# A decoder layer in split fp32: one more summed weight pair in the last gate/up block, two more in the second down block, and other pool lifetimes around them

## The chip, the cores and the metric

The kernel runs on one core of a Trainium2 chip. The metric is the device time of one execution in microseconds; "the time" below is the median of several runs, and single executions are named as such. The core has a matrix engine (PE, with its weight loads shown as PEld), a vector engine (DVE), a scalar engine (ACT), a general engine (POOL) and a sync engine (SP) that in this kernel issues most of the weight transfers.

## The reference

One layer of a hybrid decoder on 256 tokens of width 2048, all in float32:

```python
u = rmsnorm(h)
# one combined projection, then two groups of heads
lru_x, lru_gate, q, k, v, ret_gate = split(u @ w_in)
A = rg_lru(causal_conv(lru_x)) * gelu(lru_gate)
B = group_norm(retention(rope(q), rope(k), v)) * silu(ret_gate)
h = h + concat(A, B) @ w_out                         # 2048 x 2048
m = rmsnorm(h)
h = h + (silu(m @ w_gate) * (m @ w_up)) @ w_down     # d_ff = 5632, so 11 blocks of 512
out = rmsnorm(h)
```

The change touches only the last two lines of matrix products: the gate/up products and the down product.

## The kernel before, in words

**Precision.** A float32 product is made of three matmuls. Both operands are split into a high part (rounded to the matmul's own type, `F32R`) and a low part (the rest): `three` (in the functions below) adds high x high, high x low and low x high into one PSUM bank. Weights arrive raw: one transfer of 128x1024 floats (512 KB) on SP into a tile `raw`. `split` (L122 to L124) then makes two tiles of it: ACT copies it to `wh` (L123), and DVE subtracts to get `wl` (L124). Where a 512-wide half is split alone the tiles are called `bh` and `bl`. So each weight goes transfer, ACT cast, DVE subtraction, matmul.

**Quads and summed quads.** From the output projection on, the weights are worked in pairs of raw tiles, a `Quad`: a 2x2 grid of blocks `b11`, `b12` (first raw tile) and `b22`, `b21` (second), against a 2x2 grid of activations. A plain quad makes eight block products (`EIGHT`), that is 24 matmuls of 128x512. A summed quad makes seven (`SEVEN`, a scheme of the Strassen-Winograd kind), 21 matmuls; for that DVE first forms sums of weight blocks in place in the raw tiles (`add`, four additions of 128x512, L661), and more splits are made: `b11` alone, the pair `b22`/`b21`, then the two summed tiles. The activations need sums too (`Left` with `sums`: four 128x128 operations and one more split, tiles `s`, `sh`, `sl`), made once for each pair.

**Blocks.** The program is a list of steps. Blocks 0 and 1 are the output projection, 2 to 12 are gate/up, then come two down blocks. In gate/up a summed quad is cut in two steps: `s` is its shared part (class `Shared`, 4 products, 12 matmuls), which is worked during the block ahead, and `d` the rest (class `Direct`, 3 products, 9 matmuls, which loads the second raw tile of that quad once more). `p` is a plain quad and `h` half of one. `SUMMED[b]` says which of the eight quads of block b are summed, and `STEPS[b]` in which order block b takes its own steps and the `s` steps of block b+1. Each down block walks 22 quads in the order `ORDER_DOWN[d]`; those in `SUMMED_DOWN[d]` are summed.

**Buffers.** `raw` has 6 buffers, `split` 4 (each a `wh` and a `wl`), `acts` 60 tiles of 128x512 for activations. From block 3 to the start of block 12 there are two more pools: `raw2` (2 buffers, taken by each fourth raw tile) and `split2` (2, by each third split); `swap` opens them and `stop_more` ends their use. At the end of gate/up `swap_back` closes them and in their place opens `late` (4 tiles, the final norm's weights `fw`) and `resid2` (8 tiles): POOL issues eight transfers `htok<-kept_rows` (256 KB each) that bring the residual rows back, and four for `fw`.

**What sets the order.** Transfers of weights are issued on SP some loads ahead, each when its buffer is released. A scheduler that works in program order by dependencies sets the order on PE, DVE and ACT; the `end` of the second down block alone is in hand-written order on PE. Every engine then works its own list strictly in order, and waits for semaphores of the others. The first and second half of the residual rows belong to the first and second down block: `into` (L919, L920) and `post` (L941) add results to `htok`, and L984 multiplies by `fw`.

Of the kernel before, what the change touches and what calls it, by code (L numbers as in the profile page):

```python
# [9 lines left out]
F32R = mybir.dt.float32r  # L10
# [20 lines left out]

SUMMED = ((), (4, 5), (2, 3), (1, 2, 3)) + ((0, 1, 2, 3),) * 8 + ((1, 2, 3),)
SUMMED_OUT, SUMMED_FFN = (4, 5), (0, 1, 2, 3)

PLAIN = ((4, 5, 6, 7, 0, 1, 2, 3),) * 2 + (tuple(range(8)),) * 11
STEPS = ("pppspppspp", "ppspdpsdpp", "pdpsdpspspp", "pspsdpsdpsdp") + ("psdhsdhsdhsdhp",) * 7 + ("psdpsdpsddp", "psdpsdpsdpp")


EARLY_DOWN = (0, 1, 2)
SUMMED_DOWN = (9, 12, 15, 17, 19), (5, 7, 9, 11, 13, 15, 17)  # L40
ORDER_DOWN = (3, 4, 0, 5, 6, 1, 7, 8, 2) + tuple(range(9, 22)), tuple(range(22))


@with_exitstack
def tile_hymba_layer(ctx: ExitStack, tc: tile.TileContext, A: dict, out: bass.AP):
# [10 lines left out]
    tpool = early.enter_context(tc.tile_pool(name="tmp", bufs=6))  # L56
    late, resid, more, turn_of = [], [xpool], [], [0, 0]
    extra = ExitStack()
# [15 lines left out]
    def split_tiles():  # L74
        turn_of[1] += 1
        pool_ = more[1] if more and turn_of[1] % 3 == 0 else wpool
        return [pool_.tile([P, 1024], F32R, tag=g, name=nm(g)) for g in ("wh", "wl")]

    def raw_tile():
        turn_of[0] += 1  # L80
        pool_ = more[0] if more and turn_of[0] % 4 == 0 else rpool
        return pool_.tile([P, 1024], F32, tag="raw", name=nm("raw"))
# [464 lines left out]
    class Left:  # L547
# [5 lines left out]

        def __init__(self, f, sums):
            self.h, self.l = [act_tile("ah", F32R)], [act_tile("al", F32R)]
            split(self.h[0], self.l[0], f)
            if sums:
                a11, a21, a12, a22 = (f[:, n * P : n * P + P] for n in range(4))
                g = act_tile("s")
                s1, s2, s3, s4 = (g[:, n * P : n * P + P] for n in range(4))  # L560
                v.tensor_tensor(out=s1, in0=a22, in1=a21, op=ALU.subtract)
                v.tensor_tensor(out=s2, in0=a11, in1=s1, op=ALU.add)
                v.tensor_tensor(out=s3, in0=a11, in1=a21, op=ALU.subtract)
                v.tensor_tensor(out=s4, in0=a12, in1=s2, op=ALU.subtract)
                self.h.append(act_tile("sh", F32R))
                self.l.append(act_tile("sl", F32R))
                split(self.h[1], self.l[1], g)
# [49 lines left out]
    class Quad:  # L617
# [5 lines left out]
        def __init__(self, src, sums, before=None):  # L623
            self.src, self.sums, self.before = src, sums, before
            self.parts = {}
            self.apart = False

# [11 lines left out]
        def load(self, half):  # L639
            r = raw_tile()  # L640
            nc.sync.dma_start(out=r, in_=self.src[:, half * 1024 : half * 1024 + 1024])
            if half == 0 and self.before:
                self.before()
            if not self.sums:
                self.cut(("b22", "b21") if half else ("b11", "b12"), r)
                return
            if half == 0:
                self.ra = r
                self.parts["b11"] = act_tile("bh", F32R), act_tile("bl", F32R)
                split(*self.parts["b11"], r[:, :512])  # L650
                return
            self.cut(("b22", "b21"), r)
            self.add(r)
            self.cut(("t1", "t3"), self.ra)
            self.cut(("t2", "t4"), r)
# [31 lines left out]
    def block(index, quads, lefts, post, ps, tail, early={}, ordered=False):  # L687
# [39 lines left out]
        for i in range(n):  # L727
            program.append(([quads[i]], step(i)))

        def end():  # L730
# [29 lines left out]
    class Direct(Quad):  # L760
# [8 lines left out]
        def load(self, half):  # L769
            r = raw_tile()  # L770
            nc.sync.dma_start(out=r, in_=self.src[:, 1024:2048])
# [14 lines left out]
    class Block:  # L786
# [45 lines left out]
        def put(self, after):  # L832
            plain = [i for i in PLAIN[self.index] if i not in self.summed]
            for k, kind in enumerate(self.steps):
                if kind == "p":
                    i, n = plain.pop(0), len(plain)
                    quad = Quad(self.src(i), False)
                    run = lambda i=i, quad=quad, k=k, n=n: self.plain(i, quad, k == 0, n == 0)
                elif kind == "h":
# [63 lines left out]
    def make_left(p):  # L903
        if dl[p] is None:
            dl[p] = Left(ff[p], p in EARLY_DOWN + SUMMED_DOWN[0] + SUMMED_DOWN[1])

# [196 lines left out]
    def stop_more():  # L1103
        more.clear()

    def swap_back():
        extra.close()
        late.append(ctx.enter_context(tc.tile_pool(name="late", bufs=4)))
        resid[0] = ctx.enter_context(tc.tile_pool(name="resid2", bufs=8))
        for key in [(cb, t) for cb in range(4) for t in range(2)]:  # L1110
            htok[key] = res_tile("htok")
            pool.dma_start(out=htok[key], in_=kept[key])
        load_fw()

    blocks = [Block(d, lambda i, d=d: A["w_out"][8 * d + i], y, out_post(d), STEPS[d], SUMMED[d]) for d in range(2)]
# [5 lines left out]
    for b, after in zip(blocks, blocks[1:] + [down]):  # L1121
        if b.index == 3:
            program.append(([], swap))
        if b.index == NB + 1:
            program.append(([], stop_more))
        b.put(after)
    program.append(([], swap_back))

# [119 lines left out]
```

## Time and profile before

| | |
|---|---|
| time, median of 3 runs | 1083.32 us (1082.24 to 1083.6) |
| the profiled execution, its own time | 1082.46 us |
| its span, first to last instruction | 1080.7 us (so 1.76 us lie outside) |
| PE busy | 1070.2 us (99%), 5089 matmuls |
| DVE busy | 964.1 us (89%) |
| ACT busy | 664.5 us (61%) |
| POOL busy | 57.2 us (5%) |
| granted PE clock, mean | 0.998 |

A row of a timeline reads: start in us, busy time in us, engine, line, operation, output<-inputs, shapes, count, and in brackets how long the engine idled before it and what ended that. On PE successive matmuls overlap: a row's busy time is longer than the step from one start to the next. In the chain of work that ended last the times are the steps along it. Block boundaries, by the lines in the trace: the residual transfers of `swap_back` are issued from 824.9 us on, the first down block's results are added to the rows (L941) around 957 to 963 us, and the second down block runs from there to about 1070 us.

### The profile page before, as it was taken

The page shows a single profiled execution, that of the slowest core. Times are in us where ns is not written, and L with a number is a line of the kernel's source. Part 1 is how long each engine was busy: PE and PEld are TensorE (multiplying, and loading weights), DVE is VectorE, ACT ScalarE, POOL GpSimd, SP SyncE. Part 2 cuts the span into 40 slices and gives each one's busy share as a digit, 9 for nine tenths or more (in the row PEclk, how much of TensorE's full clock was granted, in tenths as well). Part 3 has the DMA queues.
Part 4 walks back from the last instruction along what each step waited for, and adds up shares of the span by engine and source line. Part 5 has one row for each costly group of instructions (what it writes and reads, how often), then busy time and mean ns, then how long its engine had stood idle before and what let it go on. Part 6 is the DMA issues. An engine that isn't in the chain of part 4 may idle for free.

```text
span 1080.7 us, 14590 instructions
## 1 busy us (share of the span) xinstructions
PE 1070.2 (99%) x5089; PEld 897.7 (83%) x5089; DVE 964.1 (89%) x1399; ACT 664.5 (61%) x947; POOL 57.2 (5%) x73
## 2 busy tenths in 40 slices
PE   9999999999999999999999999999999999999997
PEld 7888888888888888888888888888888888888886
DVE  7889789988878889989999999999999889997886
ACT  7666644468756676656656565665656656654563
POOL 0602230000000000000000000000002000000001
PEclk9999999999999999999999999999999999999999
DMA  9965475554556588677776777777767856474662
GB/s 325 336 213 171 159 254 166 183 176 158 192 195 234 183 304 273 231 235 256 257 270 228 251 260 242 263 269 232 258 234 270 289 181 214 162 245 159 214 212 101
DMA packets 71386, 244.62 MB, mean 226 GB/s; under 512 B 8208, under 2 KB 8592, under 8 KB 71312
## 3 DMA queue, kind: packets, MB, share of 16 engines
q1 hardware_dynamic: 68400, 236.34, 64.6%
q0 software_dynamic: 1472, 4.72, 1.3%
q10 hardware_dynamic: 1440, 2.62, 0.6%
q8 instruction: 40, 0.66, 0.2%
q14 instruction: 34, 0.28, 0.1%
HBM read 239.46 MB, written 4.19 MB: 225 GB/s over the span
## 4 chain that ended last, share of the span: by engine, by line
PE 98%; DVE 1%; DMA 1%; POOL 0%; SPq 0%; ACT 0%; issue 0%; POOLq 0%; ACTq 0%
PE c L685 22%; PE c L683 22%; PE c L684 22%; PE fm L194 11%; PE fm L196 5%; PE tm L174 3%; PE tm L175 3%; PE tm L176 3%; PE p L683 1%; PE p L685 1%; PE p L684 1%; PE ft L865 1%; DMA x<-in_x 1%; PE ht L588 0%; PE sc L492 0%; DVE wl L124 0%
## 5 line engine op out<-in xcount | busy, mean ns | idle before, releaser
L123 ACT CAST wh<-raw 128x1024 fp32r<-128x1024 f32 (+1 forms) x498 | 462.9, 959 | 323.8 <-PE c L685 130.8
L124 DVE TENSOR_TENSOR wl<-raw,wh 128x1024 fp32r<-128x1024 f32 (+1 forms) x498 | 542.2, 1115 | 72.5 <-ACT wh L123 71.2
L684 PE MATMUL c<-wl,ah 128*128 128x512 f32 x826 | 322.7, 391 | 0.0
L685 PE MATMUL c<-wh,al 128*128 128x512 f32 x826 | 321.8, 390 | 0.0
L683 PE MATMUL c<-wh,ah 128*128 128x512 f32 x826 | 280.3, 391 | 0.0
L683 PEld LDWEIGHTS c<-wh,ah 128*128 128x128 f32 x826 | 155.1, 188 | 32.0 <-ACT wh L123 0.3
L685 PEld LDWEIGHTS c<-wh,al 128*128 128x128 f32 x826 | 155.2, 188 | 31.8
L684 PEld LDWEIGHTS c<-wl,ah 128*128 128x128 f32 x826 | 155.2, 188 | 31.6
L194 PE MATMUL fm<-u,wh 128*128 128x512 f32 x512 | 161.4, 396 | 0.0
L196 PEld LDWEIGHTS fm<-u,wl 128*128 128x128 f32 x512 | 96.1, 188 | 22.4
L196 PE MATMUL fm<-u,wl 128*128 128x256 f32 x512 | 101.2, 279 | 0.0
L661 DVE TENSOR_TENSOR raw<-raw,raw 128x512 f32<-128x512 f32 x114 | 78.4, 689 | 2.0
L661 DVE TENSOR_TENSOR raw<-raw 128x512 f32<-128x512 f32 x114 | 78.3, 688 | 1.4
L194 PEld LDWEIGHTS fm<-u,wh 128*128 128x128 f32 x512 | 78.4, 189 | 0.3
L684 PE MATMUL c<-wl,sh 128*128 128x512 f32 x192 | 74.3, 390 | 0.0
L685 PE MATMUL c<-wh,sl 128*128 128x512 f32 x192 | 73.7, 390 | 0.0
L683 PE MATMUL c<-wh,sh 128*128 128x512 f32 x192 | 67.3, 391 | 0.3 <-ACT sh L123 0.3
L176 PE MATMUL tm<-wh,u 128*128 128x512 f32 x128 | 48.7, 391 | 0.0
L175 PE MATMUL tm<-wl,u 128*128 128x512 f32 x128 | 48.7, 393 | 0.0
L174 PE MATMUL tm<-wh,u 128*128 128x512 f32 x128 | 46.9, 394 | 1.4 <-ACT u L298 1.4
L683 PEld LDWEIGHTS c<-wh,sh 128*128 128x128 f32 x192 | 36.1, 188 | 8.1 <-ACT sh L123 0.7
L685 PEld LDWEIGHTS c<-wh,sl 128*128 128x128 f32 x192 | 36.1, 188 | 7.5
(247 smaller groups left out, 1027.4 us busy)
## 6 DMA issues: line engine op xcount, KB each, us to landing
raw<-in_w_gu SPq DMA_DIRECT2D x216, 512.0 KB, 5.3
raw<-in_w_down SPq DMA_DIRECT2D x91, 512.0 KB, 4.6
raw<-in_w_out SPq DMA_DIRECT2D x34, 512.0 KB, 3.7
raw<-in_w_lx SPq DMA_DIRECT2D x16, 512.0 KB, 6.4
raw<-in_w_k SPq DMA_DIRECT2D x16, 512.0 KB, 3.6
raw<-in_w_q SPq DMA_DIRECT2D x16, 512.0 KB, 4.2
raw<-in_w_rg SPq DMA_DIRECT2D x16, 512.0 KB, 3.5
raw<-in_w_lg SPq DMA_DIRECT2D x16, 512.0 KB, 3.5
```

What stands on the lines that cost most here:

```text
L123: act.copy(out=dst_h, in_=src)
L124: v.tensor_tensor(out=dst_l, in0=src, in1=dst_h.bitcast(F32), op=ALU.subtract)
L174: pe.matmul(ps, ah, wh, start=first, stop=False)
L175: pe.matmul(ps, ah, wl, start=False, stop=False)
L176: pe.matmul(ps, al, wh, start=False, stop=last)
L194: pe.matmul(ps, wh, hl, start=n + i == 0, stop=False)
L196: pe.matmul(ps[:, :S], wl, hl[:, :S], start=False, stop=n + i == len(order) - 1)
L661: v.tensor_tensor(out=dst, in0=a, in1=b, op=ALU.add)
L683: pe.matmul(p, ah, bh, start=first, stop=False, skip_group_check=onto)
L684: pe.matmul(p, ah, bl, start=False, stop=False, skip_group_check=onto)
L685: pe.matmul(p, al, bh, start=False, stop=last, skip_group_check=onto)
L865: pe.transpose(pt[:, o : o + P], g[:, (2 * b + c) * P : (2 * b + c) * P + P], ident)
```

## The change

It does the following.

1. The last gate/up block (12) has four summed quads in place of three; block 11 then takes four `s` steps, and block 12's steps shrink by one.
2. The second down block has nine summed quads in place of seven (12 and 19 are new), in another order: summed ones stand at positions 1, 3, 5, ... 17, plain ones between them. Before, the first five were plain and the summed ones stood at 5, 7, ... 17.
3. `raw2` is taken only by raw tiles that are split at once and not added up (`brief`: those of `Direct`, and the second raw tile of a block's last plain quad), not by each fourth. `split2` is taken as before.
4. The extra pools live longer: `stop_more` comes after step 6 of the first down block, `swap_back` after step 9.
5. The residual rows come back in two halves: `rows_back(0)`, four transfers, in `swap_back`; `rows_back(1)`, four transfers, after step 7 of the second down block. Between the two, a pool `sums` of four tiles holds the `sh` and `sl` tiles of pairs 12 and 19.

The diff, cut to its core:

```diff
-SUMMED = ((), (4, 5), (2, 3), (1, 2, 3)) + ((0, 1, 2, 3),) * 8 + ((1, 2, 3),)
+SUMMED = ((), (4, 5), (2, 3), (1, 2, 3)) + ((0, 1, 2, 3),) * 9
-STEPS = (...) + ("psdhsdhsdhsdhp",) * 7 + ("psdpsdpsddp", "psdpsdpsdpp")
+STEPS = (...) + ("psdhsdhsdhsdhp",) * 8 + ("psdpsdpsddp",)
-SUMMED_DOWN = (9, 12, 15, 17, 19), (5, 7, 9, 11, 13, 15, 17)
-ORDER_DOWN = (3, 4, 0, 5, 6, 1, 7, 8, 2) + tuple(range(9, 22)), tuple(range(22))
+SUMMED_DOWN = (9, 12, 15, 17, 19), (5, 7, 9, 11, 12, 13, 15, 17, 19)
+ORDER_DOWN = (3, 4, 0, 5, 6, 1, 7, 8, 2) + tuple(range(9, 22)), (0, 12, 1, 19, 2, 5, 3, 7, 4, 9, 6, 11, 8, 13, 10, 15, 14, 17, 16, 18, 20, 21)
+BESIDE = (12, 19)
...
-    def raw_tile():
-        turn_of[0] += 1
-        pool_ = more[0] if more and turn_of[0] % 4 == 0 else rpool
+    def raw_tile(brief=False):
+        pool_ = more[0] if more and brief else rpool
...
         def load(self, half):            # Quad
-            r = raw_tile()
+            r = raw_tile(self.brief and half == 1)
...
         for i in range(n):               # block()
             program.append(([quads[i]], step(i)))
+            if i in hooks[ordered]:
+                program.append(([], hooks[ordered][i]))
...
         def load(self, half):            # Direct
-            r = raw_tile()
+            r = raw_tile(True)
...
+                    quad.brief = n == 0  # the last plain quad of a Block
...
-            dl[p] = Left(ff[p], p in EARLY_DOWN + SUMMED_DOWN[0] + SUMMED_DOWN[1])
+            place = sum_tile if p in BESIDE else act_tile
+            dl[p] = Left(ff[p], p in EARLY_DOWN + SUMMED_DOWN[0] + SUMMED_DOWN[1], place)
...
+    def sum_tile(name, dt):
+        return sums_kept[0].tile([P, 512], dt, tag="sum", name=nm(name))
+
+    def rows_back(d):
+        resid[0] = ctx.enter_context(tc.tile_pool(name=f"resid_{d}", bufs=4))
+        for key in [(cb, t) for cb in (2 * d, 2 * d + 1) for t in range(2)]:
+            htok[key] = res_tile("htok")
+            pool.dma_start(out=htok[key], in_=kept[key])
+
     def swap_back():
         extra.close()
+        rows_back(0)
         late.append(ctx.enter_context(tc.tile_pool(name="late", bufs=4)))
-        resid[0] = ctx.enter_context(tc.tile_pool(name="resid2", bufs=8))
-        for key in [(cb, t) for cb in range(4) for t in range(2)]:
-            ...
         load_fw()
+        sums_kept.append(beside.enter_context(tc.tile_pool(name="sums", bufs=4)))
+
+    def sums_end():
+        beside.close()
+        rows_back(1)
+
+    hooks = {0: {6: stop_more, 9: swap_back}, 1: {7: sums_end}}
...
-        if b.index == NB + 1:
-            program.append(([], stop_more))
         b.put(after)
-    program.append(([], swap_back))
```

How it moves the instructions, at three places. In all, PE's list loses 9 rows and DVE's gains 19.

**Start of the second down block, DVE.** In the kernel before, quads 0, 1, 2, ... here are plain. From the split of a plain quad's raw tile (`wl_9238`) on, DVE's list reads (L941 and L984 finish the first block's residual rows):

```order
L124 TENSOR_TENSOR wl_9238<-raw_9235,wh_9237 128x1024
L984 TENSOR_TENSOR htok_8244<-htok_8244,fw_8260 128x512
L984 TENSOR_TENSOR htok_8248<-htok_8248,fw_8262 128x512
L941 TENSOR_TENSOR htok_8250<-c_1664_7918,htok_8250 128x512
L984 TENSOR_TENSOR htok_8246<-htok_8246,fw_8260 128x512
L124 TENSOR_TENSOR wl_9244<-raw_9241,wh_9243 128x1024
L124 TENSOR_TENSOR wl_9278<-raw_9275,wh_9277 128x1024
L984 TENSOR_TENSOR htok_8250<-htok_8250,fw_8262 128x512
L124 TENSOR_TENSOR wl_9284<-raw_9281,wh_9283 128x1024
```

In the changed kernel the second quad of this block is pair 12, summed: its raw tiles are `raw_9177` and `raw_9243`. Behind the split of the second one, `wl_9246`, the list reads (L945, L924 and L988 are the lines that L941, L920 and L984 were):

```order
L945 TENSOR_TENSOR htok_8644<-c_1673_7956,htok_8644 128x512
L924 TENSOR_TENSOR htok_8648<-htok_8648,part_9153 128x512
L124 TENSOR_TENSOR bl_9180<-raw_9177,bh_9179 128x512
L945 TENSOR_TENSOR htok_8648<-c_1672_7952,htok_8648 128x512
L661 TENSOR_TENSOR raw_9177<-raw_9177 128x512
L661 TENSOR_TENSOR raw_9177<-raw_9177,raw_9243 128x512
L988 TENSOR_TENSOR htok_8642<-htok_8642,fw_8653 128x512
L661 TENSOR_TENSOR raw_9243<-raw_9177,raw_9243 128x512
L988 TENSOR_TENSOR htok_8646<-htok_8646,fw_8655 128x512
L988 TENSOR_TENSOR htok_8644<-htok_8644,fw_8653 128x512
L661 TENSOR_TENSOR raw_9243<-raw_9243 128x512
L124 TENSOR_TENSOR wl_9254<-raw_9177,wh_9253 128x1024
```

Before, at most four narrow rows (128x512) stand between two wide subtractions (128x1024). Now eleven do, between `wl_9246` and the first summed tile `wl_9254`: `bl_9180` and the four additions of pair 12 stand among the rows that finish the first block. On PE, from the first use of `wl_9246` to the first use of `wl_9254`, the changed list reads:

```order
L684 MATMUL c_1979_9267<-wl_9246,ah_8672 128x512
L685 MATMUL c_1979_9267<-wh_9245,al_8673 128x512
L684 MATMUL c_1980_9271<-wl_9246,sh_8681 128x512
L685 MATMUL c_1980_9271<-wh_9245,sl_8682 128x512
L684 MATMUL p_1989_9307<-bl_9180,ah_8672 128x512
L685 MATMUL p_1989_9307<-bh_9179,al_8673 128x512
L683 MATMUL p_1990_9317<-wh_9253,sh_8681 128x512
L683 MATMUL p_1989_9307<-bh_9303,ah_9018 128x512
L684 MATMUL p_1990_9317<-wl_9254,sh_8681 128x512
```

So eight matmuls stand from the one use to the other. Before, a whole plain quad (24 matmuls for two wide subtractions) stood at this place.

**The alternation of plain and summed quads, DVE.** Before, in its steady part (from the narrow split `bl_9606` of one summed quad to `bl_9687` of the next):

```order
L124 TENSOR_TENSOR bl_9606<-raw_9603,bh_9605 128x512
L661 TENSOR_TENSOR raw_9603<-raw_9603 128x512
L124 TENSOR_TENSOR wl_9564<-raw_9549,wh_9563 128x1024
L661 TENSOR_TENSOR raw_9603<-raw_9603,raw_9630 128x512
L124 TENSOR_TENSOR wl_9570<-raw_9567,wh_9569 128x1024
L124 TENSOR_TENSOR wl_9600<-raw_9597,wh_9599 128x1024
L124 TENSOR_TENSOR wl_9633<-raw_9630,wh_9632 128x1024
L661 TENSOR_TENSOR raw_9630<-raw_9603,raw_9630 128x512
L124 TENSOR_TENSOR wl_9641<-raw_9603,wh_9640 128x1024
L661 TENSOR_TENSOR raw_9630<-raw_9630 128x512
L124 TENSOR_TENSOR bl_9687<-raw_9684,bh_9686 128x512
```

In the changed kernel, early in the block, from `bl_9389` (pair 5) to the next summed quad's `bl_9470` (pair 7); `raw_9301` and `raw_9332` are pair 19's, `raw_9350` and `raw_9380` plain pair 2's:

```order
L124 TENSOR_TENSOR bl_9389<-raw_9386,bh_9388 128x512
L661 TENSOR_TENSOR raw_9332<-raw_9332 128x512
L124 TENSOR_TENSOR wl_9343<-raw_9301,wh_9342 128x1024
L661 TENSOR_TENSOR raw_9386<-raw_9386 128x512
L124 TENSOR_TENSOR wl_9347<-raw_9332,wh_9346 128x1024
L661 TENSOR_TENSOR raw_9386<-raw_9386,raw_9413 128x512
L124 TENSOR_TENSOR wl_9353<-raw_9350,wh_9352 128x1024
L124 TENSOR_TENSOR wl_9383<-raw_9380,wh_9382 128x1024
L124 TENSOR_TENSOR wl_9416<-raw_9413,wh_9415 128x1024
L124 TENSOR_TENSOR wl_9424<-raw_9386,wh_9423 128x1024
L661 TENSOR_TENSOR raw_9413<-raw_9386,raw_9413 128x512
L124 TENSOR_TENSOR bl_9470<-raw_9467,bh_9469 128x512
```

The plain quad's first raw tile is released by `wl_9570` before and by `wl_9353` in the changed kernel, and its buffer is the one that the next summed quad's load (`raw_9684`, `raw_9467`) waits for. Before, one wide subtraction and two additions stand between the narrow split and that release; now two wide subtractions and three additions do.

**POOL's transfers.** Before, the last of the norm's weights are followed at once by all residual rows:

```order
L893 DMA fw_8264<-in_final_norm_w 128x512
L893 DMA fw_8266<-in_final_norm_w 128x512
L1112 DMA htok_8244<-kept_rows 128x512
L1112 DMA htok_8246<-kept_rows 128x512
L1112 DMA htok_8248<-kept_rows 128x512
L1112 DMA htok_8250<-kept_rows 128x512
```

In the changed kernel:

```order
L1119 DMA htok_8646<-kept_rows 128x512
L1119 DMA htok_8648<-kept_rows 128x512
L896 DMA fw_8653<-in_final_norm_w 128x512
L896 DMA fw_8655<-in_final_norm_w 128x512
L896 DMA fw_8657<-in_final_norm_w 128x512
L896 DMA fw_8659<-in_final_norm_w 128x512
L1119 DMA htok_9579<-kept_rows 128x512
L1119 DMA htok_9581<-kept_rows 128x512
```

The first four residual rows have moved ahead of the norm's weights, and the other four behind them. `htok_9579` waits on PE until the last use of the `sums` tiles, the `sl` of pair 19.

More of the change, by code (lines that the diff above doesn't have):

```diff
@@ L28 @@
 N_SMALL = 104
-SUMMED = ((), (4, 5), (2, 3), (1, 2, 3)) + ((0, 1, 2, 3),) * 8 + ((1, 2, 3),)
+SUMMED = ((), (4, 5), (2, 3), (1, 2, 3)) + ((0, 1, 2, 3),) * 9
 SUMMED_OUT, SUMMED_FFN = (4, 5), (0, 1, 2, 3)
 PLAIN = ((4, 5, 6, 7, 0, 1, 2, 3),) * 2 + (tuple(range(8)),) * 11
-STEPS = ("pppspppspp", "ppspdpsdpp", "pdpsdpspspp", "pspsdpsdpsdp") + ("psdhsdhsdhsdhp",) * 7 + ("psdpsdpsddp", "psdpsdpsdpp")
+STEPS = ("pppspppspp", "ppspdpsdpp", "pdpsdpspspp", "pspsdpsdpsdp") + ("psdhsdhsdhsdhp",) * 8 + ("psdpsdpsddp",)
 EARLY_DOWN = (0, 1, 2)
-SUMMED_DOWN = (9, 12, 15, 17, 19), (5, 7, 9, 11, 13, 15, 17)
-ORDER_DOWN = (3, 4, 0, 5, 6, 1, 7, 8, 2) + tuple(range(9, 22)), tuple(range(22))
+SUMMED_DOWN = (9, 12, 15, 17, 19), (5, 7, 9, 11, 12, 13, 15, 17, 19)
+ORDER_DOWN = (3, 4, 0, 5, 6, 1, 7, 8, 2) + tuple(range(9, 22)), (0, 12, 1, 19, 2, 5, 3, 7, 4, 9, 6, 11, 8, 13, 10, 15, 14, 17, 16, 18, 20, 21)
+BESIDE = (12, 19)
 @with_exitstack
@@ L56, in tile_hymba_layer @@
     tpool = early.enter_context(tc.tile_pool(name="tmp", bufs=6))
-    late, resid, more, turn_of = [], [xpool], [], [0, 0]
+    late, resid, more, turn_of = [], [xpool], [], [0]
     extra = ExitStack()
@@ L74, in split_tiles @@
     def split_tiles():
-        turn_of[1] += 1
-        pool_ = more[1] if more and turn_of[1] % 3 == 0 else wpool
+        turn_of[0] += 1
+        pool_ = more[1] if more and turn_of[0] % 3 == 0 else wpool
         return [pool_.tile([P, 1024], F32R, tag=g, name=nm(g)) for g in ("wh", "wl")]
-    def raw_tile():
-        turn_of[0] += 1
-        pool_ = more[0] if more and turn_of[0] % 4 == 0 else rpool
+    def raw_tile(brief=False):
+        pool_ = more[0] if more and brief else rpool
         return pool_.tile([P, 1024], F32, tag="raw", name=nm("raw"))
@@ L552, in tile_hymba_layer, with __init__ @@
         names = ("a11", "a21", "a12", "a22", "s1", "s2", "s3", "s4")
-        def __init__(self, f, sums):
+        def __init__(self, f, sums, place=act_tile):
             self.h, self.l = [act_tile("ah", F32R)], [act_tile("al", F32R)]
@@ L564, in __init__ @@
                 v.tensor_tensor(out=s4, in0=a12, in1=s2, op=ALU.subtract)
-                self.h.append(act_tile("sh", F32R))
-                self.l.append(act_tile("sl", F32R))
+                self.h.append(place("sh", F32R))
+                self.l.append(place("sl", F32R))
                 split(self.h[1], self.l[1], g)
@@ L625, in __init__ @@
             self.parts = {}
-            self.apart = False
+            self.apart = self.brief = False
         def cut(self, names, raw):
@@ L1104, in stop_more @@
         more.clear()
+    beside, sums_kept = ExitStack(), []
+    def sum_tile(name, dt):
[5 more added lines that the diff above has]
+            pool.dma_start(out=htok[key], in_=kept[key])
     def swap_back():
         extra.close()
+        rows_back(0)
         late.append(ctx.enter_context(tc.tile_pool(name="late", bufs=4)))
-        resid[0] = ctx.enter_context(tc.tile_pool(name="resid2", bufs=8))
-        for key in [(cb, t) for cb in range(4) for t in range(2)]:
-            htok[key] = res_tile("htok")
-            pool.dma_start(out=htok[key], in_=kept[key])
         load_fw()
+        sums_kept.append(beside.enter_context(tc.tile_pool(name="sums", bufs=4)))
[3 more added lines that the diff above has]
+    hooks = {0: {6: stop_more, 9: swap_back}, 1: {7: sums_end}}
     blocks = [Block(d, lambda i, d=d: A["w_out"][8 * d + i], y, out_post(d), STEPS[d], SUMMED[d]) for d in range(2)]
```

## The prediction

> **What bounds the kernel now.** I read the page's head and its chain first, to see which engine sets the end.
>
> ```profile
> span 1080.7 us, 14590 instructions
> PE 1070.2 (99%) x5089; PEld 897.7 (83%) x5089; DVE 964.1 (89%) x1399; ACT 664.5 (61%) x947; POOL 57.2 (5%) x73
> ...
> PE 98%; DVE 1%; DMA 1%; POOL 0%; SPq 0%; ACT 0%; issue 0%; POOLq 0%; ACTq 0%
> ```
>
> PE is busy 99% of the span and is 98% of the chain. The table by stage then shows whether PE waits anywhere in the region that the change touches; columns are PE, PEld, DVE, ACT and POOL busy in each 50 us, the clock, the share of the DMA engines, GB/s.
>
> ```profile
> 750.00:800.00 50.00, 50.00 (x226) 41.46 (x225) 46.27 (x57) 30.20 (x40) 0.00 (x0) 1.00 0.76 254
> 800.00:850.00 50.00, 50.00 (x226) 41.46 (x225) 47.25 (x70) 31.85 (x44) 6.39 (x12) 1.00 0.79 280
> 850.00:900.00 50.00, 50.00 (x226) 41.42 (x225) 42.84 (x67) 31.43 (x40) 0.00 (x0) 1.00 0.60 196
> 900.00:950.00 50.00, 50.00 (x222) 41.42 (x221) 47.88 (x68) 31.90 (x39) 0.00 (x0) 1.00 0.55 191
> 950.00:1000.00 50.00, 50.00 (x222) 41.44 (x221) 40.19 (x48) 24.93 (x32) 0.00 (x0) 1.00 0.56 195
> 1000.00:1050.00 50.00, 50.00 (x223) 41.42 (x222) 43.43 (x49) 27.39 (x31) 0.00 (x0) 1.00 0.64 210
> ```
>
> PE waits for nothing from 750 to 1050, at full clock. So two things follow. A matmul taken out is worth its whole step; and the change has no PE wait to remove, while every wait that it adds is a loss. DVE, at 40 to 48 of 50, is what could fall behind. How far it is ahead is read by setting a wide subtraction beside the first matmul that uses it: in each pair of rows below the first is DVE's `wl` and the second PE's first use of it, at the end of the first down block, in a plain stretch, and at two places of the alternation of plain and summed quads.
>
> ```profile
> 960.84 1.22 DVE L124 TENSOR_TENSOR wl<-raw,wh 128x1024 fp32r<-128x1024 f32 x1
> 966.78 0.39 PE L684 MATMUL c<-wl,ah 128*128 128x512 f32 x1
> ...
> 975.32 1.23 DVE L124 TENSOR_TENSOR wl<-raw,wh 128x1024 fp32r<-128x1024 f32 x1 [0.89 <-ACT wh L123]
> 982.42 0.39 PE L684 MATMUL c<-wl,ah 128*128 128x512 f32 x1
> ...
> 998.07 4.63 DVE L124 TENSOR_TENSOR wl<-raw,wh 128x1024 fp32r<-128x1024 f32 x4 [0.59 <-ACT wh L123]
> 1000.33 0.39 PE L684 MATMUL p<-wl,sh 128*128 128x512 f32 x1
> ...
> 1018.26 1.22 DVE L124 TENSOR_TENSOR wl<-raw,wh 128x1024 fp32r<-128x1024 f32 x1
> 1020.05 0.39 PE L684 MATMUL p<-wl,sh 128*128 128x512 f32 x1
> ```
>
> The lead (use minus end of the subtraction) is 966.78 - 962.06 = 4.7 us at the first, 5.9 at the second, then 1.0 (998.07 + 1.22 = 999.3, used at 1000.33) and 0.57 (1019.48, used at 1020.05). 5.9 is the most that the four `split` buffers allow: the casts there wait for PE to free one. So the alternation eats five of the six us of lead in three or four periods, and then holds at half a microsecond. What holds it is a loop through the raw buffers. The rows are from DVE's and ACT's timelines, the waits from 960 to 1050 (us in all, times, longest), and the raw loads from 1018 to 1034:
>
> ```profile
> 1009.53 3.49 DVE L124 TENSOR_TENSOR wl<-raw,wh 128x1024 fp32r<-128x1024 f32 x3
> 1016.92 0.69 DVE L124 TENSOR_TENSOR bl<-raw,bh 128x512 fp32r<-128x512 f32 x1 [1.44 <-ACT bh L123]
> 1020.00 3.49 DVE L124 TENSOR_TENSOR wl<-raw,wh 128x1024 fp32r<-128x1024 f32 x3
> 1027.06 0.69 DVE L124 TENSOR_TENSOR bl<-raw,bh 128x512 fp32r<-128x512 f32 x1 [1.11 <-ACT bh L123]
> ...
> 1016.27 0.62 ACT L123 CAST bh<-raw 128x512 fp32r<-128x512 f32 x1 [4.21 <-DMA raw<-in_w_down]
> ...
> ACT bh L123 <- DMA raw<-in_w_down: 20.9, 6, 4.2
> ...
> DMA to landing us min/median/max: 3.2/5.1/5.4
> ```
>
> The first of the three subtractions at 1009.53 ends near 1010.7 and frees a raw buffer; the load into it lands, ACT casts, and DVE takes `bl` at 1016.92, 6.2 us later, having idled 1.44. The next time it is 1021.2 to 1027.06, 5.9. I take 6.0, and as its lower end 4.9 (a landing 1.1 under the median of 5.1). From `bl` to the next release DVE has 4.2 us of work, so the loop is 10.2, just what PE needs for a plain and a summed quad: 45 matmuls by 0.227, 10.2.
>
> **The change part by part.** The steps of the engines, for the sum:
>
> ```profile
> 1058.97 0.23 PE c L685
> 1059.20 0.23 PE c L683
> 995.59 1.29 DVE L661 TENSOR_TENSOR raw<-raw 128x512 f32<-128x512 f32 x2
> ```
>
> A 128x512 matmul is a step of 0.227 (222 in 50.00 us say 0.225), a narrow DVE row 0.60 (1.29 for two that overlap, less 0.69), a wide one 1.13 ((3.49 - 1.22)/2).
>
> *Saving.* Three more summed pairs, three matmuls each: 9 x 0.227 = 2.04 us, all on the path. It is the most that the change can gain, 0.19%.
>
> *Work added.* Each new pair adds four additions and 1.5 wide splits on DVE, 4 x 0.60 + 1.5 x 1.13 = 4.1, 12.3 in all. In gate/up (item 1) blocks that have four summed pairs already run at 46.27 and 47.25 of 50 with PE full, so block 12's fourth pair costs nothing there if its steps are like theirs; its cover is the 2.7 us of spare DVE time in 50. The activations' sums of these pairs exist already. The order of the loads in the gate/up blocks hardly changes with `raw2` by kind (neighbours swap places), so that is nothing, from -0.2 to 0.2.
>
> *Place A, start of the second down block.* From `wl_9246` to `wl_9254` DVE has eleven narrow rows and a wide one, 6.6 + 1.1 = 7.7 us; PE has eight matmuls, 1.8. The lead shrinks by 5.9. With the most that buffers allow (5.9) PE waits 0.0, with the 4.7 found at this place before it waits 1.2. I take 0.6.
>
> *The first periods of the alternation.* They now begin at the block's second quad, so the plain quads that built up the lead of 5.9 are gone. From `bl_9389` to the release by `wl_9353` DVE has four narrow rows and three wide, 5.9 us (before 4.2). The loop is 4.9 to 6.0 plus 5.9, 10.8 to 11.9 against PE's 10.2: 0.1 (half a microsecond of lead left) to 1.7 (none). I take 0.6, nearer the low end, since A's wait is itself a lead for DVE. The next period has four narrow rows and two wide, 4.7 + 6.0 = 10.7: 0 to 0.5, I take 0.2; the third the same, 0.1. After that the list is the old one, and so is its price, nothing.
>
> *The second half of the rows.* Its four transfers wait on PE for the last use of pair 19's `sl`, which is within about a microsecond of when `wl_9353` releases `raw_9467`'s buffer: they share the DMA engines with the load that the loop waits for. What that costs is read where eight of them ran before:
>
> ```profile
> raw<-in_w_down SPq DMA_DIRECT2D x20, 512.0 KB, 4.6
> ...
> raw<-in_w_gu SPq DMA_DIRECT2D x5, 512.0 KB, 9.2
> raw<-in_w_down SPq DMA_DIRECT2D x4, 512.0 KB, 5.7
> htok<-kept_rows POOLq DMA_DIRECT2D x8, 256.0 KB, 8.1
> ```
>
> The first row is the stretch 1000 to 1050, the others 824 to 840. Beside eight rows (2.1 MB) a raw load took 9.2 instead of 4.6, 4.6 more; there PE did not wait, the lead covered it. Four rows are half the bytes, so 2.3 if the load meets them fully, 0 if it is ahead of them, 4.6 at the worst. I take 1.3: it is likely to meet them, with a part of the wait that DVE still covers. What is late is `bl_9470`, and behind it on DVE everything in that list; PE waits for it next.
>
> *The first half and the norm's weights,* now issued in the first down block. Summed quads follow there (DVE 47.88 of 50 from 900 on), and 42.84 before: 0 to 1.4, the latter with a full 2.3 less about 0.9 of lead; I take 0.3. Their old place at 825 had no PE wait, so moving them away gains nothing. The tail behind PE's last matmul has the same rows: 0.
>
> Sum: 0.6 + 0.6 + 0.2 + 0.1 + 1.3 + 0.3 = 3.1 us lost against 2.04 saved, +1.1. On the profiled execution's 1082.46 that is 1083.5; it lay 0.86 under the median of the runs shown, so 1084.4. The ends: everything lost at its lowest, 0.1 - 2.04 = -1.9; at its highest 1.2 + 1.7 + 0.5 + 0.5 + 4.6 + 1.4 = 9.9, +7.9.
>
> **The rivals.** *No new wait.* If DVE enters the block with its 5.9 and the loads land near 3.2, all covers hold, and the whole 2.04 is gained: 1081.3. For it: PE never waits anywhere in these 300 us, and half a microsecond of lead is enough at 1020. Against it: A takes 5.9 from a lead that stood at 4.7.
>
> *Loads delayed for as long as they meet the rows.* If four transfers delay a raw load as much as eight did (9.2 in place of 4.6, because only the time in flight together counts), the wait is 4.6 and not 1.3, and the sum +4.4: 1087.7, slower. It decides from total waits of 4.2 us on (2.04 + 0.2% of 1083). The price stands at one place, the load of `raw_9467`. For it: the eight rows landed in 8.1 at the median, so raw loads met a part of them only and still doubled. Against it: `raw<-in_w_down` in the same stretch took 5.7. [...]
>
> *The fourth pair does not fit at the end of gate/up.* Block 11 at the pattern of the others needs DVE at about 47 of 50, and block 12's steps are denser than before with a `d` more. Should DVE run over by its spare 2.7, PE would wait some 2 us there: with the rest of the sum 1086.4. Against it: eight blocks of that pattern run without a wait.
>
> **How the numbers follow.** About 0.2%, 2.2 us, is what a measurement of this kernel can tell from no change. The forecast, waits of 1.0 to 4.2 us, has 0.46 and lies within it, from 1082.3 to 1085.5. No or hardly any wait has 0.20; since the saving alone is 0.19%, half of that, 0.10, falls beyond the line by the scatter of runs, and half within. Delayed loads (0.26) and the fourth pair (0.08) are slower, 0.34. So faster 0.10, same 0.56, slower 0.34. Range: down to 1081.2, the whole saving, and up to 1087.8, the delayed load; what is left out is the upper part of the highest sums and scatter below.
>
> **What would show it.** PE should have idle time in its rows between about 960 and 1000, in two to four pieces of 0.2 to 2 us, at uses of `wl` or `bl` (released by DVE L124), and none before 850. The second group of `htok` transfers should start within 1 us of a raw load that then takes 6 to 9 us. A `bl` should idle for 2 us or more ahead of itself on DVE right after. No PE idle time there would mean the first rival; a raw landing of over 9 us with a PE gap above 3, the second; PE gaps from 770 to 850, the third. Wrong altogether would be a gain beyond 2.04, which no row of this profile can give.

## The result, and the profile after

The changed kernel takes 1097.28 us (median, 1093.88 to 1097.94), the kernel before in the same runs 1083.46: a ratio of 1.0123, 95% interval 1.01 to 1.0146. It is slower by 13.8 us, where 1084.4 was forecast (a gain of 2 us against waits of about 3), and lies outside the range. The page's head and its line of busy times:

```profile
span 1096.2 us, 14587 instructions
PE 1075.0 (98%) x5080; PEld 895.8 (82%) x5080; DVE 976.6 (89%) x1418; ACT 668.7 (61%) x954; POOL 57.2 (5%) x73
```

PE lost its nine matmuls (5089 to 5080) and is yet busy for 4.8 us more: matmuls became slower somewhere. The table by stage (columns as before: PE, PEld, DVE, ACT, POOL, clock, DMA share, GB/s) shows where:

```profile
800.00:850.00 50.00, 49.99 (x223) 40.77 (x223) 47.62 (x68) 32.65 (x44) 0.00 (x0) 1.00 0.74 249
850.00:900.00 50.00, 46.19 (x196) 37.41 (x195) 40.14 (x67) 28.24 (x40) 4.28 (x8) 0.93 0.56 192
900.00:950.00 50.00, 50.00 (x223) 41.39 (x222) 48.51 (x69) 30.75 (x39) 0.00 (x0) 1.00 0.59 198
950.00:1000.00 50.00, 46.31 (x197) 36.27 (x195) 41.68 (x51) 23.93 (x32) 2.12 (x4) 1.00 0.58 199
1000.00:1050.00 50.00, 48.07 (x207) 38.30 (x207) 43.97 (x50) 27.93 (x31) 0.00 (x0) 1.00 0.58 203
```

PE, which waited nowhere in these stretches before, idles 3.8 us from 850 to 900, at a clock of 0.93, and 5.6 us from 950 to 1050. PE's waits from 750 to 1090 (us in all, times, longest) give the releasers; before, this view was empty there:

```profile
PE c L683 <- ACT ah L123: 2.4, 1, 2.4
PE p L683 <- ACT bh L123: 2.3, 2, 1.7
PE p L683 <- ACT wh L123: 2.1, 4, 0.7
PE c L683 <- ACT c L811: 1.4, 1, 1.4
PE p L684 <- DVE wl L124: 0.7, 2, 0.5
PE c L683 <- ACT wh L123: 0.4, 2, 0.2
```

There are three places. Every step from one matmul's start to the next beyond the usual 0.227 us counts as lost.

**The end of gate/up, 6.7 us.** PE's timeline, then ACT's and the two rows of DVE's that the text needs, and a stretch of the table:

```profile
849.86 0.84 PE L685 MATMUL c<-wh,sl 128*128 128x512 f32 x3
853.08 0.50 PE L683 MATMUL c<-wh,ah 128*128 128x512 f32 x1 [2.38 <-ACT ah L123]
855.24 0.80 PE L683 MATMUL c<-wh,ah 128*128 128x512 f32 x1 [1.43 <-ACT c L811]
856.26 1.05 PE L685 MATMUL c<-wh,al 128*128 128x512 f32 x2
...
849.67 0.57 ACT L808 COPY p<-c 128x512 f32<-128x512 f32 x1
850.51 1.99 ACT L123 CAST wh<-raw 128x1024 fp32r<-128x1024 f32 x2 [0.26 <-PE c L685]
852.41 1.14 ACT L123 CAST ah<-ff 128x512 fp32r<-128x512 f32 x2
853.45 1.25 ACT L877 ACTIVATE gated<-c,r_tok 128x512 f32<-128x512 f32 x2
854.60 0.59 ACT L811 COPY c<-q 128x512 f32<-128x512 f32 x1
...
851.20 0.69 DVE L809 TENSOR_TENSOR p<-c,p 128x512 f32<-128x512 f32 x1
...
852.93 0.68 DVE L810 TENSOR_TENSOR q<-p,c 128x512 f32<-128x512 f32 x1
...
855.00:861.00 6.00, 5.76 (x14) 4.57 (x15) 3.47 (x6) 0.19 (x1) 0.00 (x0) 0.53 0.54 215
```

The matmuls at 849.86 are the last of the shared part that block 12 makes for the first down block. What they leave in the banks must go through ACT (L808), DVE (L809, L810) and ACT again (L811) before the down block adds to the same banks. In PE's list of the changed kernel the bank that L811 writes is used again after two matmuls; in the kernel before 45, most of them of block 12's last plain quads, stood between (10.2 us). The same copy there, ahead of PE's next use of the bank at 850.93:

```profile
846.42 0.58 ACT L809 COPY c<-q 128x512 f32<-128x512 f32 x1
```

It ended at 847.00, 3.9 us before it was needed. In the changed kernel it ends at 855.19 and PE takes the bank at 855.24. So the chain is bare, with two wide casts, the `ah` casts and the two rows of L877 ahead of L811 in ACT's list: 4.1 us beyond the usual steps in two waits. The first wait, at `ah`, adds nothing to the second: two matmuls later PE would have stood until L811 ended in any case. Then the clock falls to 0.53 (the window 855 to 861): the first matmul behind the second wait takes 0.60 and eleven more take 0.43 in place of 0.227, the rest, 2.6.

**The start of the second down block, 2.6 us.**

```profile
972.84 0.50 PE L683 MATMUL p<-wh,sh 128*128 128x512 f32 x1 [0.71 <-ACT wh L123]
973.98 0.50 PE L683 MATMUL p<-bh,ah 128*128 128x512 f32 x1 [0.63 <-ACT bh L123]
974.95 0.49 PE L684 MATMUL p<-wl,sh 128*128 128x512 f32 x1 [0.47 <-DVE wl L124]
...
969.90 0.63 ACT L983 ACTIVATE junk<-htok 128x512 f32<-128x512 f32 x1 [5.68 <-PE c L684]
```

This is place A of the prediction. ACT stood 5.7 us at a scratch tile, `junk`, that needs one of the 60 `acts` buffers, which PE had still to release; the cast for pair 12 is behind it in ACT's list.

**The first periods of the alternation, 6.0 us,** in some ten small waits from 985 to 1024. The largest, and the loads behind it (the DMA view of 985 to 997: KB each, median us to landing):

```profile
998.15 0.50 PE L683 MATMUL p<-bh,ah 128*128 128x512 f32 x1 [1.70 <-ACT bh L123]
...
998.13 0.69 DVE L124 TENSOR_TENSOR bl<-raw,bh 128x512 fp32r<-128x512 f32 x1 [4.41 <-ACT bh L123]
...
raw<-in_w_down SPq DMA_DIRECT2D x5, 512.0 KB, 7.5
htok<-kept_rows POOLq DMA_DIRECT2D x4, 256.0 KB, 7.9
```

The three sum to 15.3. With shorter ones, such as 0.6 from 833 to 841, all of PE's steps from 800 on lose 16.4 us; less the 2.04 saved that is 14.4, and the first row behind PE (L945) starts 14.4 later than before (1084.92 against 1070.49). The spans of the two profiled executions differ by 15.5: the last 1.1 lies behind the last rows of the engines, where the output transfers landed in 3.9 and 4.2 us (medians on SP and ACT) against 2.9 and 3.1 before.

### The profile page after: what moved, and what is told of

Same layout as the page of the kernel before. It is cut to its first block, busy times and chain, and to the rows that moved or that the text cites. A ratio compares the mean times of both kernels' runs of the same rounds, so it can differ in the third digit from the quotient of the medians.

```text
span 1096.2 us, 14587 instructions
## 1 busy us (share of the span) xinstructions
PE 1075.0 (98%) x5080; PEld 895.8 (82%) x5080; DVE 976.6 (89%) x1418; ACT 668.7 (61%) x954; POOL 57.2 (5%) x73
## 5 line engine op out<-in xcount | busy, mean ns | idle before, releaser
L684 PE MATMUL c<-wl,ah 128*128 128x512 f32 x808 | 316.4, 392 | 0.0
L685 PE MATMUL c<-wh,al 128*128 128x512 f32 x808 | 313.8, 391 | 0.0
L683 PE MATMUL c<-wh,ah 128*128 128x512 f32 x808 | 275.7, 393 | 4.3 <-ACT ah L123 2.4
L683 PEld LDWEIGHTS c<-wh,ah 128*128 128x128 f32 x808 | 152.1, 189 | 37.8 <-ACT ah L123 2.8
L685 PEld LDWEIGHTS c<-wh,al 128*128 128x128 f32 x808 | 152.3, 188 | 31.5
L661 DVE TENSOR_TENSOR raw<-raw,raw 128x512 f32<-128x512 f32 x120 | 82.7, 689 | 2.2
L661 DVE TENSOR_TENSOR raw<-raw 128x512 f32<-128x512 f32 x120 | 82.2, 687 | 1.2
L1119 POOL DMA_DIRECT2D htok<-kept_rows x8 | 4.3, 541 | 805.1 <-DVE wl L124 710.7
```

The lines of the kernel that those rows point to most:

```text
L661: v.tensor_tensor(out=dst, in0=a, in1=b, op=ALU.add)
L683: pe.matmul(p, ah, bh, start=first, stop=False, skip_group_check=onto)
L684: pe.matmul(p, ah, bl, start=False, stop=False, skip_group_check=onto)
L685: pe.matmul(p, al, bh, start=False, stop=last, skip_group_check=onto)
```

## The experiments

In each, the comparison with the kernel before is from the same chip. The changed kernel was not run again beside them; differences from its 1097.28 are good to the 0.6 us by which the medians of the kernel before differ between these series (1083.07 to 1083.61), and to the scatter of its own runs.

**Which part.** The first four take the parts apart. Gate/up as before:

```diff
-SUMMED = ... + ((0, 1, 2, 3),) * 9
-STEPS = ... * 8 + ("psdpsdpsddp",)
+SUMMED = ... + ((0, 1, 2, 3),) * 8 + ((1, 2, 3),)
+STEPS = ... * 7 + ("psdpsdpsddp", "psdpsdpsdpp")
```

> The changed kernel, with the last gate/up block as before (three summed pairs, the old steps). Theory: of the 13.8 us that the change lost, about 6.7 stand at the end of gate/up (PE waits of 2.5 and 1.6 us near 850 and then a spell of matmuls at a step of 0.43), since the last shared part now ends right ahead of the down block's first use of the same banks; here 19 matmuls stand between. So about 1097.3 - 6.7 + 0.7 (three matmuls back) = 1091.3, and no PE wait over 0.5 us and no slow matmuls from 800 to 900. Rival: the loss at 850 comes from the pools (raw2 by kind, their longer life), not from the steps; then 1097 to 1098, with the wait still there.

1088.01 us, ratio 1.0043 (1.0029 to 1.0058). The wait at 850 is gone, with its slow matmuls (granted clock 1.00 from 850 to 900), as the theory says, but the gain is 9.3 and not 6.0. The rest goes with the clock: in the profiled execution (1086.45, the fastest of five) the three waits of place A are there unchanged (0.72, 0.62, 0.48), but here the clock fell behind them, to 0.57 from 968 to 972. The slow matmuls cost 1.7 us, the lead of DVE behind them was 2.1 us where the changed kernel had 0.6, and the alternation then lost 1.0 and not 6.0. That the slow spell made this lead is likely, but no run shows it alone.

Down as before, with no pool for the sums:

```diff
-SUMMED_DOWN = ..., (5, 7, 9, 11, 12, 13, 15, 17, 19)
-ORDER_DOWN = ..., (0, 12, 1, 19, 2, 5, ...)
+SUMMED_DOWN = ..., (5, 7, 9, 11, 13, 15, 17)
+ORDER_DOWN = ..., tuple(range(22))
```

> The changed kernel, with the second down block's pairs and order as before (seven summed pairs, no pool for their sums), while the pools' lives, the two halves of the rows and gate/up stay as changed. Theory: the waits after 950 (2.6 us at the block's start, about 6 in the first four periods of the alternation) come from the summed pairs standing early and from the second half of the rows meeting a raw load. With five plain quads first the lead covers both: 1097.3 - 8.6 + 1.4 = 1090.1, with the 850 wait still there. Rival: the rows' second half costs it whatever the order: 1092 to 1094, a PE wait left near 990.

1090.36, ratio 1.0057 (1.0042 to 1.0072), the theory's number. From 950 on PE lost 0.9 us, so the rows' second half costs little behind five plain quads. The wait at 850 stands as it was.

Gate/up alone, on the kernel before:

> The kernel before, with only the last gate/up block's four pairs and steps. By its list on PE 28 matmuls (6.4 us) stand between the end of the last shared part and the first use of the bank that is copied back, against 2 in the changed kernel and 45 before. Theory (cover): the chain through ACT and DVE is mostly covered, so 1082.8 (three matmuls saved) to 1084.5. Rival (DVE cannot carry a fourth pair there): the same loss as in the changed kernel, 1083.5 - 0.7 + 6.7 = 1089.5.

1084.32, ratio 1.0006 (0.9996 to 1.0015). The cover theory: waits of 0.8 (at `al`, DVE) and 0.4 us (at `ah`, ACT) at 850, no slow matmuls (granted clock 1.00 from 850 to 900). The fourth pair as such fits, though it gains nothing: this is 1.4 above the kernel before less its three matmuls.

The last shared part one plain quad earlier (`psdpsdspddp`):

> The changed kernel, with block 12's steps psdpsdspddp in place of psdpsdpsddp: the last shared part of the down block stands one plain quad earlier, all else the same. By PE's list 26 matmuls (5.9 us) now stand between its end and the bank's next use. Theory (cover): the waits and the slow matmuls near 850 go, 1097.3 - 6.7 = 1090.6, or 1091.5 if the chain is covered only in part. Rival (DVE too full there): 1097, with the wait moved.

1094.54, ratio 1.0101 (1.0086 to 1.0116): the theory held in half. The wait at 850 and the slow matmuls are gone (granted clock 1.00 from 850 to 900), but new waits stand twenty microseconds ahead (PE's waits from 800 to 860):

```profile
PE c L684 <- DVE wl L124: 1.8, 2, 1.0
PE c L683 <- ACT sh L123: 1.5, 1, 1.5
...
```

So the part cannot simply be pulled forward here: DVE and ACT have its sums ready no sooner. Whether that is why the scheduler had put it last is not shown.

**Why gate/up alone cost so little.** In gate/up its program has the changed kernel's steps and differs from it in the pools only, yet PE's list has 28 matmuls at this place and not 2. So:

```diff
         if b.index == 3:
             program.append(([], swap))
+        if b.index == NB + 1:
+            program.append(([], stop_more))
-    hooks = {0: {6: stop_more, 9: swap_back}, ...}
+    hooks = {0: {9: swap_back}, ...}
```

> The changed kernel, but the extra pools go out of use at the start of block 12, as before (they are still closed after step 9 of the first down block). PE's list then has 25 matmuls between the end of the last shared part and the first use of the bank copied back, as in the run of gate/up alone, not 2. Theory (it is the longer life of the extra pools that makes the scheduler put the last shared part last, and the exposed chain through ACT and DVE that costs): the waits near 850 fall from 4.1 us with a slow spell to about 1.5 us without, 1097.3 - 5 = 1092.3. Rival (the fourth pair costs DVE too much whatever the pools): 1096 to 1098.

1090.16, ratio 1.0063 (1.0048 to 1.0078), 2 us better than the theory's number. The waits at 850 are 1.8 us beyond the usual steps, without a fall of the clock (1.00 from 850 to 900): 4.9 of the 6.7 are back; the other 2.2 came in the alternation, which lost 3.8 in this run's profile. PE's list at this place is that of gate/up alone, with 28 matmuls, not 25. The longer life of the extra pools let the scheduler move plain quads ahead of the shared part and so took its cover away. The 1.8 us left are not the bank's: it was copied by 853.45 and used at 854.38. They are waits for `ah` (ACT, 0.8) and `al` (DVE, 0.6), the split of the next activations.

**Place A.** The squares put later, in the kernel with gate/up as before:

```diff
-        j = act_tile("junk")
-        act.activation(out=j[:, :cw], in_=src, func=AF.Square, ...)
+        def square(): ...          # the same two lines
+        if cb >= 2: square()
...
+                defer(7 + 2 * cb + t, square)
```

> The run with gate/up as before (1088.0), with the squares of the first down block's rows (the scratch tile junk, ACT) put 7 to 10 steps later in the program. There ACT stood 5.7 us at the first of them until PE released a tile of acts, with the cast that pair 12 needs behind it in ACT's list. Theory: the wait at the start of the second down block (2.5 us in three pieces, and the slow matmuls behind it) shrinks to under 0.7, 1088.0 - 4 = 1084.0, or 1086 where the lead that the wait gave to DVE is missed afterwards. Rival (DVE's eleven narrow rows are the cause): the wait stays within 0.5 us, 1087.5 to 1088.5.

1087.9, ratio 1.0042 (1.0026 to 1.0058): the time did not move. But ACT still stands, as long as before and for the same reason; only the row has changed (ACT's timeline):

```profile
963.00 0.62 ACT L123 CAST bh<-raw 128x512 fp32r<-128x512 f32 x1 [5.68 <-PE c L684]
```

The `bh` tile of the next summed quad comes out of `acts` too, and takes the buffer that `junk` had waited for. So the run did not test what it was made for. The cast for pair 12 (`wh`) came 1.3 us earlier (963.52 against 964.85), the waits at the place are 1.9 in place of 2.5, and in this profiled execution, which at 1091.43 is 3.5 slower than the median, the next periods lose 7.4 where the run with gate/up as before lost 1.0 (PE's waits from 940 on):

```profile
PE p L683 <- ACT wh L123: 3.3, 4, 1.0
PE p L683 <- ACT bh L123: 1.4, 1, 1.4
...
```

**The second half of the rows.** Zeros in place of the four transfers, in the changed kernel:

> The changed kernel, with the second half of the residual rows set to zero by POOL instead of four transfers; this leaves part of the result out. Theory: the load of raw_9467, which took 7.7 us beside them, lands in 4 to 5; the wait of 1.9 us at 996 and a part of those that follow it (3.3 us to 1002) go, 1097.3 - 3 = 1094.3. Rival (the loop of raw buffers alone makes these waits): 1096.5 to 1098.

1095.32, ratio 1.0105 (1.0088 to 1.0122). Raw loads land in 5.4 us in place of 7.5 there, and the wait of 1.7 shrinks to nothing, but the block's other waits stay: the transfers are worth about 2.0 of the 8.6 us in this block (by the medians; the two kernels' runs overlap, 1092.07 to 1095.96 against 1093.88 to 1097.94).

**Order and buffers.** These five start from the kernel with gate/up as before. A plain quad more ahead (0, 1, 12, 2, 19, 3, 5, ...):

> The run with gate/up as before (1088.0), with a plain quad more ahead of the first summed one: the order 0, 1, 12, 2, 19, 3, 5, 4, 7, ... Pair 12's additions then no longer fall among the rows that finish the first down block. Theory (crowding at that place): its waits of 2.5 us and the slow spell shrink to below 1 us, 1084 to 1085.5. Rival (the alternation itself): the wait moves one quad on, 1087 to 1088.5.

1086.78, ratio 1.0032 (1.0022 to 1.0042), between the two numbers: fewer waits at the start (0.5 in place of 1.8), one left at `bh` (1.1), and a new one of 1.4 at the end, at 1068.56, on `bl`. Three plain quads ahead (the last summed quad then ends behind the point where bank c22 takes its rows, so that the summed quads' share of c22 is missing from the result; the work is the same, and the rows' second half comes one step later):

> The run with gate/up as before, with three plain quads ahead of the first summed one in the second down block (order 0, 1, 2, 12, 3, 19, 4, 5, ... 18, 17, 20, 21), nine summed quads as before. One plain quad first gave 1088.0, two 1086.8. Theory (each plain quad ahead gives lead back to DVE until the alternation eats it): 1085 to 1086, the waits at the block's start gone, a wait at its end instead, where now only two plain quads follow the last summed one. Rival (the number of summed quads, not their place, costs): 1086.5 to 1088.

1087.39, ratio 1.0041 (1.0027 to 1.0055). This run says most. PE's waits from 850 to the end, the row, and two of DVE's rows ahead of it:

```profile
PE c L684 <- DVE bl L124: 4.4, 1, 4.4
...
1067.44 0.68 PE L684 MATMUL c<-bl,ah 128*128 128x512 f32 x1 [4.42 <-DVE bl L124]
...
1062.37 0.69 DVE L934 TENSOR_TENSOR n<-p,part 128x512 f32<-128x512 f32 x1 [0.94 <-PE p L685]
...
1066.10 1.29 DVE L124 TENSOR_TENSOR bl<-raw,bh 128x512 fp32r<-128x512 f32 x2
```

Nine summed quads, and not one wait until 1063: with three plain quads ahead the lead carries the whole alternation. The loss is now at the end, where two plain quads follow the last summed one; the wait there was 1.4 with three and none with four. Six rows that put the last summed quad's products together stand ahead of this `bl` in DVE's list, from 1062.37 to 1066.18, and the first of them waits for PE.

The rows one by one on SP:

```diff
-            pool.dma_start(out=htok[key], in_=kept[key])    # four at once
+        nc.sync.dma_start(out=htok[cb, t], in_=kept[cb, t])   # after steps 8, 10, 12, 14
```

> The run with pair 12 one quad later (1086.8), with the four second residual rows issued one by one on SP, each two quads after the last, in place of four at once on POOL. Theory (four at once delay one raw load by some 4 us): the wait of 1.2 us at the bl of pair 7 goes, each raw load behind a row is late by 0.6 at most and the lead covers it, 1085.5. Rival (any transfer in the loop costs its bytes): 1086.5 to 1087.5, the wait spread over four places.

1085.88, ratio 1.0022 (1.0013 to 1.0032): the wait at `bh` is gone, the others stay, 0.9 faster than with the four at once, though the intervals overlap.

A seventh raw buffer in the second down block and the end of the first (a pool `raw3` of one in the place of two `fw` tiles, each seventh raw tile from it, with a break where the rows come in; the last two `fw` transfers after step 17):

> The run with pair 12 one quad later (1086.8), with a seventh raw buffer in the second down block (two of the norm's weights are loaded late instead). Theory (the loop through the raw buffers sets the pace there): with a buffer more the load of the next summed quad starts one release earlier, the narrow split's wait for its cast shrinks from 1 to 2 us to near none, and PE's waits after 970 go, 1083.5 to 1085. Rival (DVE's own work, 44 of 50 us, in its order sets it): 1086.3 to 1087.5.

1086.71, ratio 1.0036 (1.0025 to 1.0048): no faster. PE's waits from 960 to 1055 did shrink, from 2.0 to 0.5, so the loop of raw buffers is part of it; 0.6 appeared in the first down block and the end's wait stayed. Both together (the same share of c22 missing):

> Three plain quads first and the seventh raw buffer together. Theory of the loop: all waits of the block gone but the end's, 1082.5 to 1084.0, which is at or just under the kernel before. Rival: as with three plain quads alone.

1091.61, ratio 1.0075 (1.006 to 1.009), worse than either; the 4.4 us at the end are there again. By the steps of the two profiled executions it loses 3.3 more than three plain quads without the buffer: about 1.3 at waits near 936, 0.8 near 1050, and 1.2 in a longer spell of slow matmuls behind the wait at the end (granted clock 0.88 from 1050 on, against 0.90). Why they came was not settled.

**Place or number.** Eight summed quads, three plain ahead, four behind, gate/up as before:

```diff
+SUMMED_DOWN = ..., (5, 7, 9, 11, 13, 15, 17, 19)
+ORDER_DOWN = ..., (0, 1, 2, 19, 3, 5, 4, 7, 6, 9, 8, 11, 10, 13, 12, 15, 14, 17, 16, 18, 20, 21)
```

> The run with gate/up as before, with eight summed quads in the second down block (pair 12 is plain again), three plain quads ahead of the first summed one and four behind the last. PE makes three matmuls fewer than in the kernel before. Theory (place, not number: three ahead are enough for the alternation, as the run with three ahead showed, and four behind are enough for the end, as the kernel before shows): no PE wait over 0.2 us after 900, 1083.2 - 0.7 = 1082.5. Rival (one more summed quad costs as such): 1084 to 1085.5.

1082.79 against 1083.07, ratio 0.9999 (0.999 to 1.0008). The view of PE's waits from 850 on is empty, as theory says (a step near 936 is 0.2 too long):

```profile
950.00:1000.00 50.00, 50.00 (x222) 41.41 (x221) 43.90 (x54) 27.35 (x34) 2.12 (x4) 1.00 0.66 220
1000.00:1050.00 50.00, 50.00 (x222) 41.43 (x221) 44.80 (x50) 27.62 (x30) 0.00 (x0) 1.00 0.63 209
```

DVE is as busy here (43.9 and 44.8) as in the changed kernel (41.7 and 44.0): it was never short of time, only of lead. With gate/up's four pairs:

> The same second down block, with the last gate/up block's four pairs, the extra pools going out of use at block 12. Theory: the wait of 1.8 us at 850, as in the run whose extra pools end at 12, less three more matmuls: 1082.5 + 1.8 - 0.7 = 1083.6. Rival: 1085 or more.

1084.36, ratio 1.0013 (1.0004 to 1.0022): its waits at 850 (0.9) and 938 (0.6) cost more than the three matmuls give.

The rows one by one on SP, with the eight summed quads:

> Eight summed quads, three plain ahead and four behind, and the second residual rows issued one by one on SP. Theory: as without the last part, 1082.5, since the lead covers the rows' transfers in either way. Rival (the rows still delay a raw load there): 0.5 to 1.5 us faster than without.

1082.64, ratio 0.9998 (0.999 to 1.0007): the same as without. No version was measurably faster than the kernel before; what can be had is three matmuls, 0.7 us, under the 2 us that can be told apart.

## Why the prediction was wrong

**"Block 12's fourth pair costs nothing there if its steps are like theirs."** This step failed most, by 6.7 us. It was judged by DVE's spare time in 50 us, and by that measure the pair did fit: gate/up alone came to 1084.32, with only its own saving lost. But block 12's steps are not like the others'. It has eleven steps as before and not one less, with four plain quads in place of five, so after its last shared part comes one plain quad less. And the longer life of the extra pools (item 4 of the change), for which the sum has no term at all, let the scheduler use up the rest: with the pools ended at block 12 the same steps lost 1.8 there. The window of 47.25 that was read as one of the blocks with four pairs (800 to 850) is block 12 itself, with its three. The third rival put "some 2 us" here, by DVE running over its spare time; it did not (47.62 of 50 from 800 to 850). What had to be read was PE's list between the last shared matmul and the bank's next use: 2 matmuls against 45, which was there to be seen ahead of any run.

**Place A, taken as 0.6, at most 1.2; measured 2.6.** The lead on entry was 4.8, its lower case, which by itself gives 1.2. DVE's eleven narrow rows were priced about right (7.0 us against 6.6, without an idle of 1.0 for ACT among them), but ACT's list was not looked at: there ACT stood for 5.7 us at a tile of `acts`, with pair 12's cast behind it. How much of the 2.6 that made stays open, since putting the squares later only moved the stand to another row.

**The alternation and the rows, taken as 0.6 + 0.2 + 0.1 + 1.3 = 2.2; measured 6.0.** The mechanism was as described and the size was off, inside the bounds given (up to 7.3). The raw load beside the rows took 7.7, so 3.1 more than 4.6, and the rows were worth 2.0 by the run without them; the periods themselves were worth 4, not 0.9. They were entered with a lead of 0.6, and each wait seems to have been priced as if the lead had been built up again ahead of it. The collision came as named (POOL issued the four rows from 989.4 on, and `bl` then idled 4.4 on DVE). The period's rows, four narrow and three wide, are 5.8 by the prediction's own steps and not 5.9, and the delayed load gives 1087.7, not 1087.8; neither matters here.

**The first half of the rows, 0.3:** no wait from 900 to 950. **The saving, 2.04,** is in PE's list.

**The clock was not in the sum.** The prediction read "full clock" off the kernel before and priced each wait at its own length. The spell of slow matmuls added 2.6 to waits of 4.1.

Of the prediction's own signs the third rival's comes nearest to the largest loss, PE gaps at the end of gate/up, but for another reason and at three times its size; the upper end of the sum, all bounds together (+7.9), lies below the 13.8, because gate/up had next to no bound (0.2 for the loads) and the clock none.

## What to carry to other kernels

Where an engine is full and others feed it, read two distances in the lists at each place that a change reorders: how many matmuls stand between the end of a result and the next use of its bank, and how much lead the feeding engines have when a dense stretch begins and when it ends. Busy shares say little: here 44 of 50 us on DVE was enough with three plain quads ahead and four behind, and cost microseconds with one ahead or two behind. More buffers are not neutral under a scheduler: they change what it moves forward, and so what covers what.

## What the runs showed of the hardware

In this kernel some waits cost more than themselves. In the changed kernel, after waits of 2.4 and 1.4 us at 850 with two matmuls between them, the granted clock was 0.53 from 855 to 861, and matmuls stepped by 0.43 us in place of 0.227. The clock fell there in the two other runs with the same gate/up and pools: with down as before, with the same two waits (2.4 and 1.4), it was 0.97 from 850 to 900, and with the rows not loaded, where PE idled 3.3 us in that stretch, 0.93, as in the changed kernel. It fell too after the 4.4 us at the end of the run with three plain quads ahead (0.83 from 1062 to 1072, steps of 0.43). The three waits of place A, 0.7, 0.6 and 0.5 within 3 us, lowered the clock in the run with gate/up as before (0.57 from 968 to 972) and did not in the changed kernel (1.00 from 960 to 980) or the run with the pools ended at 12 (1.00 from 950 to 1000), with waits of like size; nor did the 1.7 at 998 in the changed kernel (1.00 from 950 to 1050). So the length of a wait alone does not tell whether the clock falls behind it; what does is not shown by these runs.
